# Query, key and value blocks in fp16 pairs by seven products, and the output projection in fp16

## The chip, the cores and the metric

The kernel runs on one core of a Trainium2 chip. The metric is the device time of one execution in microseconds. Of three runs of the kernel before, the median is 2335.99 us.

## What is computed

One layer of a decoder trunk for 512 tokens of 2048 features in f32: a token mixer (sparse attention with 16 heads in 4 groups), a squared-ReLU feed-forward part, a gated per-layer embedding add and a final norm. What matters here is the mixer:

```python
hn   = rms_norm(h, norm_mix)
proj = hn @ w_in          # q (16 x 128), kc, vc, ks, vs, kw, vw (4 x 128 each), 48 gates
k_cmp, v_cmp = compress(kc, ...), compress(vc, ...)      # silu(blk @ w1) @ w2
# for each head: three softmaxes over the same q: compressed, selected, window
out  = g0 * o_c + g1 * o_s + g2 * o_w
h    = h + out @ w_out
h    = h + (relu(rms_norm(h) @ ffn_w1) ** 2) @ ffn_w2    # 2048 -> 8192 -> 2048
h    = h + (p @ ple_w_proj) * sigmoid(rms_norm(h) @ ple_w_gate)
y    = rms_norm(h, norm_final)
```

With 512 tokens all eight selectable key blocks are selected, so the selected branch is causal attention over all tokens.

## The kernel before

Every product of f32 matrices is made from two halves of each factor, a high half (the value rounded to a shorter type) and a low half (what is left): `mm3` (L73) issues three matmuls, high by high, high by low and low by high, into one PSUM bank. Activations are kept transposed, features on partitions, so that a matmul has a 128x128 weight tile and up to 512 token columns. The type of the halves differs by stage:

- Attention stage, to about 850 us: halves in fp32r. `unit` (L105) loads a megabyte of weights (128 x 2048) and `halves` (L93) splits it; the high half is made on ScalarE (L79) and the low half on VectorE or, after the first projections, on GpSimd (L80, `lo_eng`).
- Feed-forward and embedding stages: halves in fp16, both scaled by a power of two that `scale_of` (L662) takes from a sum of squares (L676), made by `scaled_split` (L678). From the third group on, two blocks of `ffn_w1` are multiplied at once: a 2x2 partition of weights and inputs needs seven products of half-size blocks in place of eight (`PAIR`, `up_pair` L975), with 256 token columns in each matmul. `combos` (L942) makes the sums of input quarters, `prepare` (L716) those of the weights.

The attention stage runs so. The compression columns of keys (c = 0) and of values (c = 1) are projected first, 192 matmuls of 512 columns each, while the input is loaded, normed and split (`norm_split`, tiles ah and al, L160). Then follows one stream of jobs, made by `later_jobs` (L449): the compression itself (`cjob`, 130 columns), the gates, key and value blocks of each group and query blocks of each head (`block_job` L303, 48 matmuls into one bank, then `k_evac`, `v_evac` or `q_evac`), and output projections (`out_half` L290: 8 output tiles from two heads, each added to h at L299). `merge` (L472) interleaves that stream with the attention of the heads: `s_stage` (L333: scores, softmax, four row tiles; the first tile in the bank s1, the others in the bank pair s2) and `pv_stage` (L406: probabilities are transposed, split into th and tl, and multiplied with the values). A head's output oh, ol stands in fp32r.

In the later stages the weights are fed by a pump: `pump` (L753) is called after each used weight slot and decides on what is staged (loaded), squared, scaled and split next; RAWS = 6 raw buffers of 512 KB, SLOTS = 9 pairs of halves, `lags` the numbers of pumps between staging and squaring or scaling.

All this sets an order of priority. The order of each engine's instructions is then fixed when the program is built, by a planner that takes what is ready first (`TileContext(..., schedule_with_timeline_sim=True)`), so a later instruction can stand ahead of an earlier one that isn't ready. Engines run their instructions in that fixed order.

Of the kernel before, what the change touches and what calls it, by code (L numbers as in the profile page):

```python
# [31 lines left out]
SLOTS = 9  # L32
STD = 2
# [8 lines left out]
def trunk_kernel(ctx, tc, xT, pT, gains, w_kcvc, w_blk, w_gates, w_out, w1c, w2c, posT,  # L42
# [10 lines left out]
    wraw = a_sb.enter_context(tc.tile_pool(name="wraw", bufs=2))  # L53
    wsp = a_sb.enter_context(tc.tile_pool(name="wsp", bufs=3))
# [27 lines left out]
    lo_eng = [DVE]  # L82

# [9 lines left out]
    def halves(r, cols=2048, step=1024, pool=None, tags=("wh", "wl")):  # L93
        res = []
        for c in range(0, cols, 1024):
# [3 lines left out]
            for d in range(0, n, step):  # L99
                e = min(n, d + step)  # L100
                split(hi[:, d:e], lo[:, d:e], r[:, c + d:c + e], lo_eng[0])
# [11 lines left out]
    aconst = a_sb.enter_context(tc.tile_pool(name="aconst", bufs=1))  # L113
# [14 lines left out]
    wb = consts.tile([128, S], BF16, name="wb")  # L128
# [93 lines left out]
    def norm_scale(tag):  # L222
        rs = actp.tile([128, S], F32, name="rs", tag="rs")
        ACT.activation(rs, norm_bcast(tag), AF.Copy)
        return rs
# [20 lines left out]
    def gemm_k(o, hs, k, n=128):  # L246
        wh, wl = wslice(hs, k * n, n)
        mm3(o, wh, wl, ah[k], al[k], k == 0, k == NK - 1)

    warm = bank("pt")  # L250
    for i in range(WARM):
        mm(warm, wb[:, (i % 4) * 128:(i % 4 + 1) * 128], wb, True, True)
    kvp = a_sb.enter_context(tc.tile_pool(name="kv", bufs=1))
    A = {}

    def k_evac(o, rs, g, b, last):
        if b == 0:
            A["kx", g] = [kvp.tile([128, 1088], F32R, name=f"kx{e}", tag=f"kx{e}") for e in range(2)]
        kx = A["kx", g]
        t = tmp.tile([128, S], F32, name="kt", tag="t")  # L260
        DVE.tensor_mul(t, o, rs)
        for j in range(2):
            c0 = 32 + 544 * j
            d = [x[:, c0:c0 + 512].rearrange("p (j b n) -> p j b n", j=2, b=2)[:, :, b, :] for x in kx]
            split(d[0], d[1], t[:, j * 256:(j + 1) * 256].rearrange("p (j n) -> p j n", j=2))
# [5 lines left out]
    def v_evac(o, rs, g, b):  # L271
        t = tmp.tile([128, S], F32, name="vt", tag="t")
        DVE.tensor_mul(t, o, rs)
        vp = bank("pt")
        for i in range(4):
            nc.tensor.transpose(vp[:, i * 128:(i + 1) * 128], t[:, i * 128:(i + 1) * 128], ident)
        vh = kvp.tile([128, S], F32R, name="v_h", tag=f"vh{b}")
        vl = kvp.tile([128, S], F32R, name="v_l", tag=f"vl{b}")
        split(vh, vl, vp)
        A["vx", g, b] = (vh, vl)  # L280

    def q_evac(o, rs, hd):
        t = tmp.tile([128, S], F32, name="qt", tag="t")
        DVE.scalar_tensor_tensor(t, o, QSCALE, rs, op0=OP.mult, op1=OP.mult)
        qh = kvp.tile([128, S], F32R, name="q_h", tag="qh", bufs=2)
        ql = kvp.tile([128, S], F32R, name="q_l", tag="ql", bufs=2)
        split(qh, ql, t)
        A["q", hd] = (qh, ql)

    def out_half(pair, u, hs):  # L290
        os = [A["o", 2 * pair + e] for e in range(2)]
        for j in range(8):
            m = u * 8 + j
            o = bank("g")
            for e in range(2):
                wh, wl = wslice(hs, e * 1024 + j * 128)
                mm3(o, wh, wl, os[e][0], os[e][1], e == 0, e == 1)
                yield
            DVE.tensor_add(h[m], h[m], o)  # L299
            if pair == HEADS // 2 - 1:  # L300
                norm_sq(m, 12)

    def block_job(blk, evac, *a):  # L303
        def run(hs):
            o = bank("g")
            for k in range(NK):
                gemm_k(o, hs, k)
                if k == NK - 1:
                    evac(o, *a)
                yield  # L310
        return (lambda: unit(w_blk[blk]), run)

    def kjob(g, b):
# [935 lines left out]
```

## Time and profile before

| what | value |
|---|---|
| median of three runs | 2335.99 us (2334.61 to 2338.15) |
| the profiled execution, its own time | 2335.97 us |
| span of the profiled execution | 2334.0 us |
| TensorE busy | 2303.0 us |
| VectorE busy | 1562.6 us |
| ScalarE busy | 1285.7 us |
| GpSimd busy | 301.2 us |
| mean granted clock of TensorE | 0.995 |

PE is TensorE, PEld its weight load, DVE VectorE, ACT ScalarE, POOL GpSimd, SP the engine that issues the transfers. Times are from the start of the span. Busy times are unions of the records of one engine; the record of a matmul includes its way through the array, so that records of successive matmuls overlap, and the rate is read from the distance of their starts or from the length of a stretch. A name such as `wl<-raw,sc,wh` gives the tile written and those read; "idle before, releaser" says how long an engine stood idle before the group's instructions and who ended it.

### The profile page before, as it was taken

The page shows a single profiled execution, that of the slowest core. Times are in us where ns is not written, and L with a number is a line of the kernel's source. Part 1 is how long each engine was busy: PE and PEld are TensorE (multiplying, and loading weights), DVE is VectorE, ACT ScalarE, POOL GpSimd, SP SyncE. Part 2 cuts the span into 40 slices and gives each one's busy share as a digit, 9 for nine tenths or more (in the row PEclk, how much of TensorE's full clock was granted, in tenths as well). Part 3 has the DMA queues.
Part 4 walks back from the last instruction along what each step waited for, and adds up shares of the span by engine and source line. Part 5 has one row for each costly group of instructions (what it writes and reads, how often), then busy time and mean ns, then how long its engine had stood idle before and what let it go on. Part 6 is the DMA issues. An engine that isn't in the chain of part 4 may idle for free.

```text
span 2334.0 us, 35213 instructions
## 1 busy us (share of the span) xinstructions
PE 2303.0 (99%) x14042; PEld 1640.7 (70%) x14042; DVE 1562.6 (67%) x2752; ACT 1285.7 (55%) x2125; POOL 301.2 (13%) x161
## 2 busy tenths in 40 slices
PE   9999999999999989999999999999999999999997
PEld 7888888888888768577657766775677567644445
DVE  6447646646646958876777777677767776766733
ACT  5324434334333648576566656665666576565851
POOL 0243233232332120000000000000000000002012
PEclk9999999999999999999999999999999999999998
DMA  5232122222121413233233323333333233341411
GB/s 202 104 120 73 55 73 73 70 75 73 62 84 67 159 55 128 73 118 120 89 109 111 117 99 109 109 109 100 118 109 109 94 115 118 109 154 55 147 53 73
DMA packets 59061, 232.51 MB, mean 100 GB/s; under 512 B 6928, under 2 KB 7312, under 8 KB 51728
## 3 DMA queue, kind: packets, MB, share of 16 engines
q1 hardware_dynamic: 58896, 230.25, 29.4%
q8 instruction: 110, 1.80, 0.3%
q14 instruction: 55, 0.45, 0.1%
HBM read 223.94 MB, written 6.29 MB: 99 GB/s over the span
## 4 chain that ended last, share of the span: by engine, by line
PE 91%; DVE 4%; ACT 2%; DMA 2%; issue 1%; POOL 0%; SPq 0%; DVEq 0%; ACTq 0%; POOLq 0%
PE g_ps L71 50%; PE pt_ps L71 31%; PE s_ps L71 5%; PE o_ps L71 3%; PE pt_ps L427 1%; ACT s_ps L676 1%; DVE wl L683 1%; DVE xt L891 1%; DMA raw<-in_w_pg_dram 1%; ACT wh L682 1%; DMA raw<-in_ffn_dram 1%; DVE xgl L896 0%; PE pt_ps L419 0%; DVE p L384 0%; POOL fo L1178 0%
## 5 line engine op out<-in xcount | busy, mean ns | idle before, releaser
L71 PEld LDWEIGHTS <-wh 128*128 128x128 f16 x6336 | 609.0, 98 | 335.5 <-issue 8.8
L683 DVE SCALAR_TENSOR_TENSOR wl<-raw,sc,wh 128x1024 f16<-128x1024 f32 x266 | 341.6, 1288 | 188.3 <-ACT wh L682 184.5
L71 PEld LDWEIGHTS <-wl 128*128 128x128 f16 x3168 | 309.2, 98 | 174.4 <-issue 3.5
L676 ACT ACTIVATE s_ps<-raw 128x1024 f32<-128x1024 f32 x294 | 300.5, 1022 | 138.8 <-DMA raw<-in_ffn_dram 104.5
L682 ACT ACTIVATE wh<-raw,sc 128x1024 f16<-128x1024 f32 x266 | 298.5, 1139 | 90.0 <-PE g_ps L71 54.4
L80 POOL TENSOR_TENSOR wl<-raw,wh 128x1024 fp32r<-128x1024 f32 x100 | 240.6, 2411 | 506.0 <-ACT wh L79 496.0
L79 ACT ACTIVATE wh<-raw 128x1024 fp32r<-128x1024 f32 (+1 forms) x122 | 125.6, 1044 | 221.8 <-PE g_ps L71 160.1
L179 POOL TENSOR_TENSOR ssacc<-ssacc,sq 128x512 f32<-128x512 f32 x35 | 46.2, 1319 | 1428.8 <-issue 1289.8
L71 PE MATMUL g_ps<-ah,wh 128*128 128x512 f32 x544 | 215.4, 396 | 0.0
L71 PE MATMUL g_ps<-ah,wl 128*128 128x512 f32 x544 | 214.2, 394 | 0.0
L71 PE MATMUL g_ps<-al,wh 128*128 128x512 f32 x544 | 212.9, 391 | 0.0
L71 PE MATMUL pt_ps<-fh,wh 128*128 128x512 f16 (+1 forms) x544 | 203.1, 373 | 0.0
L71 PE MATMUL g_ps<-fh,wh 128*128 128x512 f16 (+1 forms) x544 | 203.0, 373 | 0.0
L71 PE MATMUL pt_ps<-fl,wh 128*128 128x512 f16 (+1 forms) x544 | 203.0, 373 | 0.0
L71 PE MATMUL g_ps<-fl,wh 128*128 128x512 f16 (+1 forms) x544 | 202.9, 373 | 0.0
L71 PE MATMUL g_ps<-fh,wl 128*128 128x512 f16 (+1 forms) x544 | 202.9, 373 | 0.0
L71 PE MATMUL pt_ps<-fh,wl 128*128 128x512 f16 (+1 forms) x544 | 202.8, 373 | 0.0
L683 DVE SCALAR_TENSOR_TENSOR wl<-S,sc,wh 128x1024 f16<-128x1024 f32 x112 | 143.6, 1282 | 76.1 <-ACT wh L682 73.4
L682 ACT ACTIVATE wh<-S,sc 128x1024 f16<-128x1024 f32 x112 | 127.5, 1139 | 72.2 <-PE pt_ps L71 39.6
L377 ACT ACTIVATE p<-s_ps,nm 128x128 f32<-128x128 f32 (+3 forms) x128 | 66.3, 523 | 116.2 <-DVE scm L373 57.3
L71 PE MATMUL pt_ps<-xcl,wh 128*128 128x256 f16 x448 | 122.2, 273 | 0.0
L71 PE MATMUL pt_ps<-xch,wh 128*128 128x256 f16 x448 | 122.1, 273 | 0.0
(286 smaller groups left out, 4880.7 us busy)
## 6 DMA issues: line engine op xcount, KB each, us to landing
raw<-in_ffn_dram SPq DMA_DIRECT2D x256, 512.0 KB, 3.8
raw<-in_w_blk_dram SPq DMA_DIRECT2D x32, 1024.0 KB, 4.8
raw<-in_w_out_dram SPq DMA_DIRECT2D x16, 1024.0 KB, 4.8
raw<-in_w_pg_dram SPq DMA_DIRECT2D x32, 512.0 KB, 3.8
h<-in_xT_dram SPq DMA_DIRECT2D x16, 256.0 KB, 6.6
raw<-in_w_kcvc_dram SPq DMA_DIRECT2D x4, 1024.0 KB, 4.8
raw<-in_w1c_dram SPq DMA_DIRECT2D x4, 1024.0 KB, 4.8
raw<-in_w_kcvc_dram SPq DMA_DIRECT2D x6, 512.0 KB, 6.3
```

Of the source, the lines that this page charges most:

```text
L71: nc.tensor.matmul(o, w, x, start=start, stop=stop, skip_group_check=True)
L79: ACT.activation(hi, src, AF.Copy)
L80: (eng or DVE).tensor_sub(lo, src, f32(hi))
L179: (DVE if e else eng or POOL).tensor_add(acc[e], acc[e], sq)
L377: ACT.activation(p, v[:, b], AF.Exp, bias=nm[:, b:b + 1], accum_out=r[:, b:b + 1])
L427: nc.tensor.transpose(pt[:, (i - kc) * 128:(i - kc + 1) * 128], A["P", hd, b, i, kc], ident)
L676: ACT.activation(junk, src, AF.Square, accum_out=sq)
L682: ACT.activation(hi[:, cs], src[:, cs], AF.Copy, scale=sc)
L683: DVE.scalar_tensor_tensor(lo[:, cs], src[:, cs], sc, hi[:, cs], op0=OP.mult, op1=OP.subtract)
L891: DVE.scalar_tensor_tensor(t, h[k], P["gx"][:, i, k:k + 1], rs, op0=OP.mult, op1=OP.mult)
```

## The change

- **Pairs.** The 32 key, value and query blocks are taken two at a time (`pair_job`): kk, vv and qq jobs, each by seven products of 256 token columns in fp16, as `up_pair` does. Products x and y go to the two g banks, v and u to the bank s1. The scale of the weights and of the norm's gain is taken out in the eviction.
- **Input quarters.** `pair_inputs` makes the fp16 halves of the input's quarters and of their combinations (7 pairs of tiles for each of 8 pairs of k-tiles) and writes them over ah and al, once the projection of c = 1 and the gates have read those. To free them in pairs, that projection runs over k in the order 0, 8, 1, 9, ... (`ORDER`), with the gates four k-tiles behind (`GLAG`).
- **Output projection.** `out_job` multiplies four heads at a time, in fp16: 4 jobs for each group, 4 output tiles in each, 4 x 3 matmuls into one bank, one scaled addition to h. oh and ol are written in fp16, with a scale from the values' squares (`o_scale`). The jobs of a group run beside the heads of the next; those of the last group come last.
- **Feed.** The pump becomes a class `Feed` with two instances: FF for the later stages as before, FA for attention (5 raw buffers, 4 slots, lags 1 and 3, sums of weights written in place). A pump of FA takes scales only where `scale` is true. `scale_of` takes one matmul and a VectorE sum in place of a matmul for each column.
- **Places.** All low halves are made on VectorE (`lo_eng` goes). The first score tile moves from bank s1 to s2. The first feed-forward weights are prepared beside the last group's output jobs.

```diff
+RAWS_A = 5
+SLOTS_A = 4
+LAGS_A = (1, 3)
+GLAG = 4
+ORDER = [k for p in range(8) for k in (p, p + 8)]
...
+    def scale_of(sq, n=1, pool=None):
...
+        mm(p[:, 0:c * n], wb, sq, True, True)
...
+        if c > 1:
+            src = pool.tile([128, 2], F32, name="se", tag="se")[:, 0:n]
+            DVE.tensor_reduce(src, p[:, 0:c * n].rearrange("p (c n) -> p n c", n=n), AX.X, OP.add)
...
+            for name in PAIR:
+                if self.inplace:
+                    if name == "S2":
+                        s1 = tile_s("S1")
+                        DVE.tensor_add(s1, a21, a22)
+                        DVE.tensor_add(a21, a21, a11)
+                        DVE.tensor_add(a11, a11, s1)
+                        S_.update({"S2": a11, "s3": a21})
+                    elif name == "S1":
+                        DVE.tensor_add(a12, a12, a11)
+                        S_["s4"] = a12
...
+                if scale and n < self.squared and self.pumps - items[n].at >= lags[1]:
+                    items[n].sc, items[n].inv = scale_of(items[n].sq, 1, self.p["sm"])
...
+    FA = Feed(PA, RAWS_A, SLOTS_A, True)
+    FA.lags = LAGS_A
...
+    def out_job(g, u):
+        it = FA.add(Item(w_out[g, u]))
...
+            for j in range(4):
+                m = 4 * u + j
+                o = bank("g")
+                for e in range(HPG):
...
+                    mm3(o, wh[:, ws], wl[:, ws], oh, ol, e == 0, e == HPG - 1)
...
+                DVE.scalar_tensor_tensor(h[m], o, iv, h[m], op0=OP.mult, op1=OP.add)
...
+    def pair_job(blk, evac, a0, a1, qs=1.0):
+        it = FA.add(Item(w_blk[blk], w_blk[blk + 1]))
...
+            def prod(b, w, x, first):
+                if first:
+                    o[b] = bank("g" if b in "xy" else "s1")
+                wh, wl = it.w[w]
+                for k in range(8):
...
+                    mm3(o[b][:, 0:H2], wh[:, ws], wl[:, ws], xh, xl, first and k == 0, k == 7)
...
+            yield from prod("x", "11", "11", True)
+            keep(1)
+            FA.used(False)
...
+            yield from prod("v", "12", "21", True)
+            total(0, 0, 1, "v")
+            FA.used(False)
...
+            yield from prod("x", "S2", "t2", False)
+            keep(2)
+            FA.used()
...
+            yield from prod("y", "S1", "t1", True)
+            FA.used()
...
+            yield from prod("x", "s3", "T3", False)
+            keep(3)
+            total(1, 1, 3, "y")
+            FA.used(False)
...
+            yield from prod("u", "22", "T4", True)
+            total(1, 0, 3, "u")
+            FA.used(False)
...
+            yield from prod("y", "s4", "22", False)
+            total(0, 1, 2, "y")
+            FA.used()
...
             if i == 0:
-                s = bank("s1")
+                s = sbank()
...
-        split(oh, ol, oc)
+        oh = opool.tile([128, S], F16, name="oh", tag=f"oh{hd % HPG}")
+        ol = opool.tile([128, S], F16, name="ol", tag=f"ol{hd % HPG}")
+        scaled_split(oh, ol, oc, A["osc", g][:, 0:1])
...
+    def pair_inputs(k):
+        ta, tb = xt(0, k, rs, tmp), xt(0, k + 8, rs, tmp)
...
+        xsplit(dh[:, 0], dl[:, 0], ta[:, 0:H2])
+        xsplit(dh[:, 1:3].rearrange("p a b -> p (a b)"), dl[:, 1:3].rearrange("p a b -> p (a b)"), tb)
+        cm = PA["S"].tile([128, 4, H2], F32, name="cm", tag="S")
+        combine(cm, ta, tb, ch, cl)
...
+    jobs = [kk_job(0), qq_job(0), vv_job(0)]
+    for g in range(GROUPS):
+        more = g + 1 < GROUPS
+        kinds = ["q2", 0, 1, "k", 2, "q4", "v", 3]
...
+    jobs += [out_job(GROUPS - 1, u) for u in range(4)]
...
+    merge([(s_stage(0, (pp, small)), 5)], 28, fill)
...
+        if r == HPG - 1 and more:
+            merge([(pvg, 10)], 28, fill)
+            flush()
+            merge([(s_stage(hd + 1, (pp, small)), 5)], 28 + no, fill)
+            flush()
         else:
...
+            gens = [(pvg, 10)] + ([(s_stage(hd + 1, (pp, small)), 5)] if hd + 1 < HEADS else [])
+            merge(gens, no + (28 if r == 0 else 14 if more else 0), fill)
...
+    merge([(early(12, 5), 12)], 64, fill)
```

## Rows read from the trace of the kernel before

**Rows 1.** Page, first section: busy us (share of span) and instructions.

```profile
PE 2303.0 (99%) x14042; PEld 1640.7 (70%) x14042; DVE 1562.6 (67%) x2752; ACT 1285.7 (55%) x2125; POOL 301.2 (13%) x161
```

**Rows 2.** Table by stage: length; busy PE, PEld, DVE, ACT, POOL; clock, DMA share, GB/s.

```profile
51.00:180.00 129.00, 129.00 (x682) 109.82 (x682) 57.16 (x83) 42.63 (x59) 48.93 (x21) 1.00 0.29 102
304.57:480.81 176.24, 176.23 (x882) 148.27 (x881) 108.34 (x218) 64.60 (x144) 57.77 (x25) 1.00 0.21 72
...
0.00:850.00 850.00, 838.93 (x4204) 699.64 (x4205) 523.57 (x1022) 345.05 (x700) 259.34 (x123) 1.00 0.26 90
```

**Rows 3.** Chain of waits in order of time: start, length, what.

```profile
108.06 5.31 PE s_ps L71 x48
...
362.28 12.05 PE g_ps L71 x53
...
938.37 0.03 PE s_ps L71 x2
938.39 10.50 PE g_ps L71 x96
...
2254.59 20.72 PE g_ps L71 x96
```

**Rows 4.** Groups of PE by line and shape: count, busy us, mean ns, idle before.

```profile
L71 PE MATMUL g_ps<-ah,wh 128*128 128x512 f32 x544 | 215.4, 396 | 0.0
...
L71 PE MATMUL g_ps<-ol,wh 128*128 128x512 f32 x256 | 100.4, 392 | 0.0
...
L71 PE MATMUL s_ps<-sq,wb 128*128 128x1 bf16 x310 | 36.4, 166 | 2.5 <-ACT s_ps L676 2.3
```

**Rows 5.** Timeline of 776 to 784 us: start, length, engine, line, operation.

```profile
776.98 4.78 POOL L80 TENSOR_TENSOR wl<-raw,wh 128x1024 fp32r<-128x1024 f32 x2 [15.61 <-ACT wh L79]
...
779.63 2.74 DVE L384 TENSOR_SCALAR p<-p,r,gate 128x384 f32<-128x384 f32 x2
...
783.08 1.27 DVE L299 TENSOR_TENSOR h<-h,g_ps 128x512 f32<-128x512 f32 x2
```

**Rows 6.** Groups of DVE by line and shape, from 845 us on.

```profile
L683 DVE SCALAR_TENSOR_TENSOR wl<-raw,sc,wh 128x1024 f16<-128x1024 f32 x257 | 330.4, 1288 | 188.1 <-ACT wh L682 184.3 <-PE g_ps L71 1.8
L1074 DVE SCALAR_TENSOR_TENSOR h<-g_ps,iv,h 128x512 f32<-128x512 f32 x128 | 95.4, 745 | 28.5 <-PE g_ps L71 28.5
...
L997 DVE TENSOR_TENSOR ft<-z,g_ps 128x256 f32<-128x256 f32 x84 | 32.4, 413 | 10.8 <-PE g_ps L71 9.2 <-PE s_ps L71 1.6
L669 DVE TENSOR_SCALAR e<-s_ps 128x1 int32<-128x1 int32 x131 | 19.7, 151 | 63.9 <-PE s_ps L71 63.9
```

**Rows 7.** Groups of DVE and POOL by line and shape, up to 845 us.

```profile
L299 DVE TENSOR_TENSOR h<-h,g_ps 128x512 f32<-128x512 f32 x126 | 84.9, 679 | 18.0 <-PE g_ps L71 17.8
L80 DVE TENSOR_TENSOR q_l<-qt,q_h 128x512 fp32r<-128x512 f32 x16 | 32.6, 2037 | 7.4 <-ACT q_h L79 7.4
...
L80 DVE TENSOR_TENSOR tl<-pt_ps,th 128x512 fp32r<-128x512 f32 x32 | 21.9, 685 | 9.7 <-ACT th L79 9.7
...
L80 POOL TENSOR_TENSOR wl<-raw,wh 128x1024 fp32r<-128x1024 f32 x100 | 240.6, 2411 | 506.0 <-ACT wh L79 496.0 <-PE g_ps L71 10.0
```

**Rows 8.** Groups of ACT by line and shape, up to 845 us.

```profile
L682 ACT ACTIVATE wh<-raw,sc 128x1024 f16<-128x1024 f32 x9 | 9.9, 1140 | 0.8 <-DVE sc L670 0.8
```

**Rows 9.** Page, DMA issues: count, KB each, median us from issue to landing.

```profile
raw<-in_ffn_dram SPq DMA_DIRECT2D x256, 512.0 KB, 3.8
```

**Rows 10.** Table by stage of four short stretches, columns as in the second group.

```profile
700.00:750.00 50.00, 50.00 (x261) 42.58 (x260) 39.06 (x89) 20.88 (x53) 13.50 (x6) 1.00 0.14 44
900.00:950.00 50.00, 49.61 (x454) 43.59 (x453) 45.99 (x96) 37.88 (x66) 0.00 (x0) 1.00 0.32 107
815.00:820.00 5.00, 2.31 (x11) 1.47 (x10) 5.00 (x6) 2.85 (x5) 0.00 (x0) 1.00 0.10 29
820.00:825.00 5.00, 5.00 (x20) 3.21 (x21) 0.07 (x2) 1.19 (x2) 0.00 (x0) 0.66 0.53 190
```

**Rows 11.** Waits of PE: line, who for, us in total, times, longest.

```profile
PE o_ps L71 <- DVE tl L80: 4.7, 3, 1.9
```

More of the change, by code (lines that the diff above doesn't have):

```diff
@@ L280, in v_evac @@
+        scaled_split(vh, vl, vp, sc)
         A["vx", g, b] = (vh, vl)
[L282 to L287, printed above, removed]
-        A["q", hd] = (qh, ql)
[L290 to L294, printed above, removed]
-            for e in range(2):
[L296 to L313, printed above, removed]
-        return block_job(g * 8 + b, k_evac, A["rs"], g, b, b)
-    def vjob(g, b):
-        return block_job(g * 8 + 2 + b, v_evac, A["rs"], g, b)
-    def qjob(hd):
-        return block_job((hd // HPG) * 8 + 4 + hd % HPG, q_evac, A["rs"], hd)
@@ L333, in s_stage, with kk_job, vv_job, qq_job @@
+    def kk_job(g):
+        return pair_job(g * 8, k_evac, (g, 0), (g, 1))
+    def vv_job(g):
+        return pair_job(g * 8 + 2, v_evac, (g, 0), (g, 1))
+    def qq_job(hd):
+        return pair_job((hd // HPG) * 8 + 4 + hd % HPG, q_evac, (hd,), (hd + 1,), QSCALE)
+    def stream(jobs):
+        for run in jobs:
+            yield from run()
     def s_stage(hd, pools):
@@ new lines, in trunk_kernel @@
+    hs = unit(w1c[1, 0])
+    for i in range(NK - GLAG, NK):
+        gate_step(i)
+    keep_kv(1, pss)
+    for i in range(NK - GLAG + 1, NK, 2):
+        pair_inputs(ORDER[i] - 8)
+    FA.pump()
+    compress(1, 0, hs)
+    hs = unit(w1c[1, 1])
+    compress_out(0)
+    gt = tmp.tile([128, S], F32, name="gt", tag="t")
+    DVE.tensor_mul(gt[0:96], gp[0:96, 0:S], rs[0:96])
+    FA.pump()
+    compress(1, 1, hs)
+    gates_out(gt)
+    compress_act(1)
+    for _ in range(12):
+        next(fill, None)
@@ L651, in trunk_kernel @@
+    compress_out(1)
+    c_sb.close()
+    P["kv"] = a_sb.enter_context(tc.tile_pool(name="kv", bufs=1))
+    for _ in range(16):
+        next(fill, None)
+    flush()
     pp = a_sb.enter_context(tc.tile_pool(name="pp", bufs=2))
@@ L674, in sum_sq @@
-    def sum_sq(junk, src, sq):
-        with nc.allow_low_precision(reason="a power of two is taken from it"):
-            ACT.activation(junk, src, AF.Square, accum_out=sq)
-    def scaled_split(hi, lo, src, sc, step=1024):
-        n = src.shape[-1]
-        for c in range(0, n, step):
-            cs = slice(c, min(n, c + step))
-            ACT.activation(hi[:, cs], src[:, cs], AF.Copy, scale=sc)
-            DVE.scalar_tensor_tensor(lo[:, cs], src[:, cs], sc, hi[:, cs], op0=OP.mult, op1=OP.subtract)
@@ L742, in trunk_kernel @@
             ms = [ffn1[G * FG + j] for j in range(FG)]
[L743 to L744 removed]
+            for it in [Item(a) for a in ms] if G < STD else [Item(*ms[0:2]), Item(*ms[2:4])]:
+                FF.add(it)
         if G > 0:
[L746 to L748 removed]
@@ L826, in trunk_kernel, with early @@
-    lo_eng[0] = POOL
-    merge([(s_stage(0, (pp, small)), 5)], counts[-1], fill)
+            for c in range(4):
+                FF.add(Item(ffn2[G - 1, c]))
+    for it in [Item(pT), Item(w_proj[1])] + [Item(w_pg[m]) for m in range(NK)]:
+        FF.add(it)
+    pump, used, take = FF.pump, FF.used, FF.take
+    def early(n0, n1):
+        FF.limit = n1
+        for n in range(n0):
+            FF.pump((1, 2))
+            yield
+    for _ in range(28):
+        next(fill, None)
+    flush()
@@ L925, in trunk_kernel @@
         for k in range(NK):
-            t = xt(0, k, rs)
+            t = xt(1, k, rs)
             if k < 8:
```

810 lines of the change are left out of this document (429 added, 381 removed).

## The prediction

> **What bounds the kernel now.** I read the page's first section, then the table by stage, then the chain of waits, then the groups of instructions on TensorE, VectorE and ScalarE. TensorE is busy 2303.0 of 2334.0 us [rows 1]. The part that the change rewrites is the attention stage, the first 850 us: TensorE works there for 838.9 us of 850, VectorE for 523.6 us, GpSimd for 259.3 us, and in a whole cycle of four heads (304.57 to 480.81) TensorE never waits while VectorE is busy 61% of the time [rows 2]. So time is saved by taking work from TensorE, as long as VectorE, which gets all that is added, keeps up. That is the whole question here: TensorE's saving is nearly certain, what is given back in waits isn't. The profiled execution took 2335.97 us, 2.0 more than its span, and the median is 2335.99; the sum below is a difference to either.
>
> **TensorE's work.** The rate is read from uninterrupted stretches of the chain, since the mean of a matmul's record includes its pipeline. 53 fp32r matmuls of 512 columns took 12.05 us, 0.2274 us each; 96 in fp16 of 512 columns 20.72 us, 0.2158 us each; 96 in fp16 of 256 columns 10.50 us, 0.1094 us each; 48 of 130 fp32r columns 5.31 us, 0.1106 us each [rows 3].
> - Query, key and value blocks: 32 blocks of 16 k-tiles by 3 matmuls are 1536 fp32r matmuls (three groups of 544, less the 32 of each that belong to the compression columns [rows 4]), 1536 x 0.2274 = 349.3 us. After: 16 pairs by 7 products by 8 k-tiles by 3 = 2688 matmuls of 256 columns, x 0.1094 = 294.1 us. Gain 55.2 us: 12.5% of it from seven products in place of eight, the rest from fp16.
> - Output projection: 768 matmuls (256 each of three groups [rows 4]) stay 768. 768 x (0.2274 - 0.2158) = 8.9 us.
> - Scales: 310 matmuls of one column [rows 4] become one for each scale, some 136 in the feed-forward stages and 39 new ones in attention. Two stretches of the chain are 0.03 us apart where two of them stand between [rows 3], so each costs between 0.015 and 0.1 us; at 0.025 the 135 fewer give 3.4 us (2 to 13).
> Attention itself, the compression and the gates have the same matmuls.
>
> The Trainium skill has a rule against halving the columns: TensorE: Matmul & The Clock Gate, section "Back-to-back issue gap", gives a sustained 131 ns for 512 columns and 81 ns for 128, hence, as an estimate on a line between, 98 ns for 256. By it the blocks would go from 201 to 263 us and the change would lose 62 us there. The trace disagrees: 0.2158 and 0.1094 us, a ratio of 0.51 [rows 3], so that of the rule only the mild form in the third rival is left.
>
> **VectorE's work in the attention stage.** Successive operations overlap by some 0.08 us (two of 0.68 us took 1.27 [rows 5]), so I take 0.08 off each mean [rows 6, 7].
> - A pair: 7 low halves of 1024 columns (1.288 - 0.08) and 4 sums of 1024, which I take as a little less (1.14), 4 totals of 256 (0.413 - 0.08), scale and factors about 0.45 (0.151 each less the overlap): 8.5 + 4.6 + 1.3 + 0.45 = 14.8 us, 16 times: 237 us [rows 6].
> - An output item: 2 low halves, 4 additions of 0.745, small ones: 5.5 us, 16 times: 88 us; 128 additions to h at 0.60 go: -77 us. The 32 scalings of evicted blocks go: -19 us [rows 6, 7].
> - Input quarters (pair_inputs), 8 times: two scaled copies of 512 (as the addition of 0.745), splits of 256, 512, 768 and 256 columns, four combinations of 256 (0.413): 1.3 + 2.2 + 1.3 = 4.8 us, together 39 us [rows 6].
> - Low halves of the compression weights move from GpSimd: 8 x 1.2 = 9 us.
> - GpSimd's 100 subtractions of 2411 ns go from this stage, and with them a collision: q_l, with both inputs in SBUF, took 2037 ns, tl of the same size but with one input in PSUM 685 [rows 7]; while GpSimd worked from 776.98 on, p took 2.74 us for two [rows 5]. For q_l alone this is 16 x 1.35 = 22 us; over all groups of such operations some 80 us, an estimate (22 to 90).
> The sum: 523.6 + 237 + 88 - 77 - 19 + 39 + 9 - 80 and some small ones = about 715 us, while TensorE's becomes 838.9 - 55.2 - 8.9 + 1 = 776 us. VectorE goes from 62 to 92% of TensorE's time. ScalarE's added work (1.140 us for each high half, about as much for each square [rows 8]) makes it some 75% busy and isn't the bound.
>
> On the collision the Trainium skill, GPSIMD Engine Reference, section "Key points", says that GpSimd shares its SBUF interfaces with VectorE and collides with instructions of two SBUF inputs or a two-port mode. By that rule the 80 is right rather than the 22, as p and the small vectors would be freed too.
>
> **Where TensorE will wait.**
> 1. *The start.* From 51 us on, TensorE has 192 x 0.2274 + 32 x 0.2274 (gates) + 192 x 0.1106 (compression) = 72 us until the first pair. In that time VectorE must make the quarters (39), 16 low halves (19), the two evictions of compression inputs (10), activations, gates and the first two weight slots (about 9): 77 us at least. The last eviction, two of the eight pair_inputs and the last compression weights all come after the last projection matmul, when TensorE has only about 12 us left to cover 17 to 20. Before, nothing waited here (129.00 of 129.00 [rows 2]). I take 13 us, bounds 4 and 20.
> 2. *The end of each pair.* The scale of the next item may only be taken in pumps with `scale` true and three pumps after it was staged; it is staged after the second product (before that the five raw buffers are full), so the first such pump is the one after the seventh product. All weights of the pair are used by then. Then the chain stands bare: scale matmul 0.2, four small VectorE operations 0.6 (0.151 each), the high half 1.14, the low half 1.29: 3.2 us [rows 4, 6, 8]. Sixteen pairs: 51 us if nothing covers it, 0 if attention's matmuls, which are merged into the same stream, always do. The trace of before has no such place, as its weights lie up to nine slots ahead. Five ends have little attention queued (the first two pairs, and the last query pair before each value pair, where the scores wait for that query's own eviction): 5 x 3.2 = 16 us. At the other eleven about 1.9 us of ready attention work stands in the queue: 11 x 1.3 = 14 us. I take 30, the middle of the bounds for the reason given. The load isn't on this chain: 5 products are 13 us, and four transfers of 512 KB, 3.8 us from issue to landing [rows 9], overlap.
> 3. *The clock.* In 815 to 820 TensorE worked 2.31 of 5 us, and in the next 5 us its granted clock was 0.66 [rows 10], a mean of the levels 2.4 and 1.2 GHz, so 1.7 us were lost. Waits of 3 us should do this at some of the sixteen places: I take 5 us (0 to 27).
> 4. *Thin heads.* Heads 13 to 15 get one output item each (48 x 0.2158 = 10.4 us) beside them, and all four score tiles now share one bank pair: 3 us (0 to 8).
> 5. *Waits that go.* The waits for tl, 4.7 us in three, the longest 1.9 [rows 11], come from VectorE late by the collision (p's 2.74 us stands right before that one [rows 5]): -5 us (-6 to 0). The feed-forward stages and the end keep their order; hence nothing.
>
> Sum: -55.2 - 8.9 - 3.4 + 13 + 30 + 5 + 3 - 5 = -21.5 us, 2314.5 us.
>
> **Rivals.**
> *The waits are covered.* The order of instructions is made by readiness, so later attention work can fill the 3.2 us gaps; VectorE's idle time in a cycle of four heads is 176.24 - 108.34 = 68 us now [rows 2], which speaks for it. Then only 5 us of the start and 2 of the thin heads stay: -67.5 - 5 + 7, 2270 us. Against it: the first two pairs have no attention beside them at all. Chance 0.22.
> *VectorE becomes the bound: slower.* It must do 715 us in order while TensorE's waits depend on it. The point of decision is the share at which it can be kept busy: at 715/850 = 0.84 the stage is as long as before. The best 50 us of before are 45.99, or 0.92, in the feed-forward stage, which speaks against; the best within attention are 39.06, or 0.78 [rows 10], though VectorE waited for TensorE there. At 0.82 the stage takes 872 us: +22, less 3.4, about 2354 us. Chance 0.18.
> *The fp16 products don't run at their rate between fp32r matmuls.* If each costs half an fp32r matmul, 0.1137 us [rows 3], the blocks gain 43.7 and the output little: the sum is some -1, 2335 us. The mixed stretches of attention, where 512-column fp32r matmuls keep to 0.23 us, speak against. Chance 0.07.
>
> **How the numbers follow.** The forecast, 2314, has 0.53, with 2297 to 2333 as its own range. The range of all: the covered case lies at 2270, with half of its chance above 2275, and a mild case of the VectorE bound ends at 2348: 2275 to 2348. A measurement tells 0.2% (4.7 us) from no change, so "same" is 2331.3 to 2340.7. Faster: 0.47 of the forecast, the 0.22, 0.02 of the VectorE case, 0.02 of the third: 0.73. Slower: 0.01 of the forecast, 0.14 of the VectorE case, 0.02 of the third: 0.17. Same: the rest, 0.10.
>
> **What would show it.** Right: 2688 matmuls of 256 columns 0.109 us apart; VectorE 700 to 730 us busy in the attention stage; TensorE idle 2 to 4 us before the first product of pairs, on VectorE's wl or ScalarE's wh, and some 10 us before the first pair; q_l back at about 0.7 us; cycles of four heads of 160 to 170 us in place of 176.2. Wrong: TensorE's idle time within 10 us of before (the gaps were covered), or waits for tl and the score tiles spread over all heads (VectorE's queue is the bound), or a feed-forward cycle that differs from 78.5 us by more than 1 us.

## Result and the profile after

| | before | after |
|---|---|---|
| median, us (four runs each) | 2335.84 | 2353.39 (2351.41 to 2354.33) |
| ratio to before, 95% interval | | 1.0071 (1.0058 to 1.0084) |
| span of the profiled execution, us | 2334.0 | 2351.0 |
| mean granted clock | 0.995 | 0.981 |

The change makes the kernel 0.7% slower; forecast were 2314 us and a range that ended at 2348. The page's first section after, to be read against [rows 1]:

```profile
PE 2270.4 (97%) x15094; PEld 1558.6 (66%) x15094; DVE 1756.5 (75%) x3345; ACT 1487.2 (63%) x2474; POOL 60.1 (3%) x61
```

TensorE is busy 32.6 us less, and yet the end comes 17 us later. To see how much of its busy time is work, I took the distance from each matmul's start to the next one's in both traces, and its median for each form at the full clock. Median times count is the time that the work needs; the rest of the distances is idle time, what is lost while the granted clock is at 1.2 GHz, and small delays of matmuls that overlap their neighbours' records:

| us, whole trace | before | after | difference |
|---|---|---|---|
| work at the full clock | 2286.3 | 2219.4 | -66.9 |
| TensorE idle | 21.5 | 71.3 | +49.8 |
| lost at the low clock | 6.2 | 33.3 | +27.1 |
| small delays | 9.8 | 17.1 | +7.3 |

So the matmuls save what was forecast (-67.5), and 84 us come back as waits and clock, where 46 were forecast. The table by stage after shows where (columns as in [rows 2]):

```profile
100.00:121.00 21.00, 14.38 (x65) 11.11 (x63) 19.58 (x42) 10.98 (x18) 0.00 (x0) 0.88 0.15 50
121.00:172.00 51.00, 40.07 (x278) 32.52 (x278) 38.74 (x76) 22.16 (x38) 0.00 (x0) 0.81 0.14 42
172.00:205.00 33.00, 25.06 (x192) 20.01 (x193) 20.94 (x35) 17.24 (x27) 0.00 (x0) 0.90 0.21 64
205.00:480.00 275.00, 262.40 (x1964) 211.85 (x1962) 245.38 (x542) 185.24 (x385) 0.00 (x0) 0.97 0.22 68
480.00:700.00 220.00, 213.36 (x1539) 162.93 (x1537) 185.48 (x399) 144.17 (x287) 0.00 (x0) 0.97 0.25 79
700.00:800.00 100.00, 99.95 (x624) 67.65 (x623) 83.85 (x205) 63.98 (x132) 0.00 (x0) 1.00 0.33 111
800.00:900.00 100.00, 87.79 (x491) 53.23 (x491) 62.57 (x129) 63.08 (x112) 15.64 (x12) 0.93 0.20 69
...
0.00:850.00 850.00, 795.37 (x5347) 612.05 (x5348) 702.22 (x1492) 542.84 (x1042) 14.35 (x20) 0.96 0.28 91
```

Of the 84 us, 39 arise between 100 and 205 us, where before nothing waited: idle 25.5, clock 11.3, small delays 2.8. Another 32 arise from 205 to 800 us, 6.5 from 800 to 900, and some 6 in the feed-forward and embedding stages, of which the forecast said nothing. VectorE is busy 702.2 of the first 850 us, 523.57 before [rows 2].

What TensorE waits for, first from 100 to 205 us, then ("...") from 205 to 700 us (who for: us in total, times, longest):

```profile
PE g_ps L80 <- ACT wh L285: 6.7, 3, 4.3
PE g_ps L80 <- DVE c L551: 4.8, 2, 2.9
PE s_ps L80 <- DVE vst L829: 3.7, 1, 3.7
PE s_ps L80 <- DVE kcmp L89: 2.6, 1, 2.6
...
PE s_ps L80 <- ACT p L642: 6.4, 6, 3.9
PE pt_ps L692 <- DVE v_l L286: 2.6, 2, 1.5
PE o_ps L80 <- ACT th L88: 1.9, 3, 1.0
PE g_ps L80 <- ACT wh L285: 1.6, 2, 0.8
...
PE s_ps L80 <- ACT wh L285: 1.2, 3, 0.4
```

There is no one waiter: the pair's weights (wh), the pair's totals (c), the compression's last copies (vst, kcmp) and attention's own steps (p, th, v_l) are all late at times. The compression's small steps stand one behind the other across three engines: from 150 to 172 us TensorE waits 6.9 us while VectorE itself is busy less than half of the time:

```profile
150.00:172.00 22.00, 15.07 (x98) 11.17 (x95) 10.38 (x26) 8.42 (x19) 0.00 (x0) 0.84 0.21 71
```

The end of the first pair (its product u comes last there), from the timeline (start, length, engine, line, operation, idle before and its releaser), is the bare chain that was forecast:

```profile
170.70 0.31 PE L80 MATMUL s_ps<-xch,wl 128*128 128x256 f16 x1
171.04 0.42 DVE L551 TENSOR_TENSOR c<-zs,s_ps 128x256 f32<-128x256 f32 x1 [4.55 <-PE s_ps L80]
...
171.52 0.16 PE L80 MATMUL s_ps<-sq,wb 128*128 128x4 bf16 x1 [0.51 <-DVE c L551]
171.72 0.16 DVE L265 TENSOR_REDUCE se<-s_ps 128x1 f32<-128x4 f32 x1 [0.25 <-PE s_ps L80]
...
172.51 0.14 DVE L268 TENSOR_SCALAR sc<-e 128x1 int32<-128x1 int32 x1
172.63 2.19 ACT L285 ACTIVATE wh<-raw,sc 128x1024 f16<-128x1024 f32 x2 [0.62 <-DVE sc L267]
...
173.83 0.28 PE L80 MATMUL g_ps<-xdh,wh 128*128 128x256 f16 x1 [2.15 <-ACT wh L285]
```

From 171.01, the end of the pair's last matmul, to 173.83 TensorE does one scale matmul and waits 2.7 us. The scale matmul itself waits for the total c, since both use the bank s1.

The clock, in five short stretches (columns as above):

```profile
117.00:122.00 5.00, 0.62 (x3) 0.13 (x2) 5.00 (x13) 3.99 (x4) 0.00 (x0) 0.50 0.00 0
293.00:297.00 4.00, 2.30 (x14) 1.57 (x13) 3.44 (x14) 2.69 (x11) 0.00 (x0) 1.00 0.00 0
297.00:300.00 3.00, 3.00 (x13) 2.76 (x13) 2.47 (x8) 2.21 (x3) 0.00 (x0) 0.51 0.02 5
498.00:502.00 4.00, 2.68 (x13) 1.64 (x13) 4.00 (x9) 2.85 (x7) 0.00 (x0) 0.55 0.02 4
502.00:506.00 4.00, 4.00 (x23) 2.99 (x23) 4.00 (x8) 2.19 (x2) 0.00 (x0) 0.59 0.00 0
```

From 293 to 297 us TensorE waited 0.71, 0.58 and 0.41 us, no wait of a whole microsecond; the clock fell to 1.2 GHz at 297.1 and stayed there for 3.4 us, in which TensorE worked without a pause. At 498.4 us it fell after waits of 0.16, 0.61 and 0.26 us in the 2.8 us before, and stayed low for 6.8 us; the waits of 0.80 and 0.43 us in the row from 498 us came with and after the fall. In the first 900 us there are 16 such stretches, 75 us together; before there were two.

### The profile page after: what moved, and what is told of

Same layout as the page of the kernel before. It is cut to its first block, busy times and chain, and to the rows that moved or that the text cites. A ratio compares the mean times of both kernels' runs of the same rounds, so it can differ in the third digit from the quotient of the medians.

```text
span 2351.0 us, 38233 instructions
## 1 busy us (share of the span) xinstructions
PE 2270.4 (97%) x15094; PEld 1558.6 (66%) x15094; DVE 1756.5 (75%) x3345; ACT 1487.2 (63%) x2474; POOL 60.1 (3%) x61
## 4 chain that ended last, share of the span: by engine, by line
PE 75%; DVE 12%; DMA 6%; ACT 4%; issue 3%; POOL 0%; ACTq 0%; DVEq 0%; POOLq 0%
PE g_ps L80 36%; PE pt_ps L80 30%; PE s_ps L80 5%; DVE wl L286 3%; DMA raw<-in_w_blk_dram 3%; PE o_ps L80 2%; ACT wh L285 1%; DMA raw<-in_ffn_dram 1%; DMA raw<-in_w_pg_dram 1%; ACT s_ps L273 1%; DMA raw<-in_w_out_dram 1%; DVE xt L740 1%; DVE nm L636 1%; PE pt_ps L692 1%; DVE p L649 1%
## 5 line engine op out<-in xcount | busy, mean ns | idle before, releaser
L80 PEld LDWEIGHTS <-wh 128*128 128x128 f16 x8640 | 839.2, 99 | 464.4 <-issue 29.0
L286 DVE SCALAR_TENSOR_TENSOR wl<-raw,sc,wh 128x1024 f16<-128x1024 f32 x394 | 505.0, 1285 | 192.6 <-ACT wh L285 186.7
L80 PEld LDWEIGHTS <-wl 128*128 128x128 f16 x4320 | 425.6, 99 | 225.6 <-issue 8.1
L285 ACT ACTIVATE wh<-raw,sc 128x1024 f16<-128x1024 f32 x394 | 442.1, 1140 | 132.1 <-PE g_ps L80 69.0
L80 PE MATMUL g_ps<-xch,wh 128*128 128x256 f16 x832 | 226.8, 273 | 0.0
L80 PE MATMUL g_ps<-xcl,wh 128*128 128x256 f16 x832 | 226.6, 273 | 0.0
L80 PE MATMUL g_ps<-xch,wl 128*128 128x256 f16 x832 | 225.2, 273 | 0.0
L273 ACT ACTIVATE junkA<-raw 128x1024 bf16<-128x1024 f32 x96 | 101.4, 1057 | 76.0 <-DMA raw<-in_w_blk_dram 49.2
L80 PE MATMUL pt_ps<-xch,wl 128*128 128x256 f16 x448 | 122.1, 272 | 0.0
L1219 DVE SCALAR_TENSOR_TENSOR h<-g_ps,iv,h 128x512 f32<-128x512 f32 x128 | 95.4, 745 | 25.0 <-PE g_ps L80 25.0
```

Of the source, the lines that this page charges most:

```text
L80: nc.tensor.matmul(o, w, x, start=start, stop=stop, skip_group_check=True)
L273: ACT.activation(junk, src, AF.Square, scale=sc, accum_out=sq)
L285: ACT.activation(hi[:, cs], src[:, cs], AF.Copy, scale=sc)
L286: DVE.scalar_tensor_tensor(lo[:, cs], src[:, cs], sc, hf, op0=OP.mult, op1=OP.subtract)
L1219: DVE.scalar_tensor_tensor(h[m], o, iv, h[m], op0=OP.mult, op1=OP.add)
```

## Experiments

Differences in this table are to the kernel after, from the ratios: (ratio - 1.0071) x 2336 us. The interval of a single ratio is 0.0010 to 0.0022 to either side, 2.3 to 5 us; with the kernel after's own interval a difference is uncertain by 4 to 6 us.

| run | ratio to before | us against after |
|---|---|---|
| e1_const: fixed weight scale | 0.9979 (0.9970 to 0.9989) | -21.5 |
| e2_flag6: scale one product earlier | 1.0103 (1.0087 to 1.0120) | +7.5 |
| e3_quarters: seven of eight pair_inputs left out | 1.0045 (1.0030 to 1.0060) | -6.1 |
| e4_nolow: no low halves of the weights | 0.9957 (0.9943 to 0.9972) | -26.6 |
| e5_start: other bank, two buffers | 1.0064 (1.0049 to 1.0079) | -1.6 |
| e6_junk: squares to SBUF | 1.0157 (1.0142 to 1.0172) | +20.1 |
| e8_fill: 224 idle matmuls added | 1.0092 (1.0075 to 1.0109) | +4.9 |
| e9_nosq: e1 without squares | 0.9944 (0.9924 to 0.9963) | -29.7 |
| e10_all: e9 and e4 | 0.9810 (0.9793 to 0.9826) | -61.0 |
| e11_all_q: e10 and e3 | 0.9763 (0.9749 to 0.9778) | -71.9 |
| e12_pact: e9, softmax scaling on ScalarE | 0.9932 (0.9911 to 0.9954) | -32.5 |
| e14_nop: no softmax scaling | 1.0035 (1.0024 to 1.0047) | -8.4 |

### The scale chain

```diff
+                if hasattr(self, "fixed") and n < self.staged:
+                    items[n].sc, items[n].inv = self.fixed[:, 0:1], self.fixed[:, 1:2]
+                    self.scaled += 1
+                    continue
```

> The kernel after, but the attention stage's weights (pairs and output items) take a fixed scale of 64 in place of the one from their squares; the squares are still made, only the scale matmul and its four VectorE operations of each item are left out, so a weight slot can be split as soon as its load has landed. Theory 1 (the chain scale, high half, low half stands bare at the end of each pair and at the start): the waits of 0.6 to 4 us before the first products of a pair go, and with them most of the 75 us at the low clock: 30 to 45 us less, 2308 to 2323 us. Theory 2 (the start is bound by VectorE, the pair ends cost little): -3 to -12 us, 2341 to 2350. Theory 3 (VectorE's queue as a whole is the bound): only 32 times 0.6 us of VectorE's work go, most of it hidden: -5 to -15 us, 2338 to 2348.

Measured: 2330.61 us, 21.5 us less. The chain costs time, half to three quarters of the 30 to 45 us that the theory of bare chains expected. Its profiled execution took 2337.70 us, 7 more than its median, so its trace isn't read for shares. It does show that the waits of the start changed their names here too: from 100 to 205 us none for wh is left, and the longest two are for the compression's copies:

```profile
PE g_ps L80 <- DVE kct L787: 8.7, 1, 8.7
PE s_ps L80 <- DVE vst L836: 4.8, 1, 4.8
```

```diff
             total(1, 0, 3, "u")
-            FA.used(False)
+            FA.used()
```

> The kernel after, with one flag changed: a scale may also be taken in the pump after a pair's sixth product, so that the chain of the next pair starts one product (24 matmuls, 2.6 us) earlier; the same work. Theory 1: the bare chain of 3.2 us at a pair's end gets 2.6 us of cover; at 16 ends -10 to -30 us with the clock that comes back, 2323 to 2343 us. Theory 2: only the ends in the start matter, -2 to -5 us, about 2350. Theory 3: within 4 us of the kernel after, since VectorE's work is the same.

Measured: 2360.90 us, slower, which no theory expected. From 200 to 900 us TensorE now waits for zs, ScalarE's copy of product x out of its bank, 6.2 us (the kernel after: 0.7 us):

```profile
PE g_ps L80 <- ACT zs L548: 6.2, 6, 2.0
```

Ahead of each of the six, ScalarE runs a high half of later weights (wh) or a square (junkA) and goes on to zs without a pause; here at one of the two longest:

```profile
521.42 2.18 ACT L285 ACTIVATE wh<-raw,sc 128x1024 f16<-128x1024 f32 x2
523.50 1.05 ACT L273 ACTIVATE junkA<-raw 128x1024 bf16<-128x1024 f32 x1
...
524.53 0.37 ACT L548 ACTIVATE zs<-g_ps 128x256 f32<-128x256 f32 x1
```

So work for later weights stands ahead of zs in ScalarE's fixed order; this is some 5 of the 9.4 us that TensorE idles more from 205 to 700 us (PE 466.33 us busy for 475.75). That the earlier scale put it there fits, but no run tests it. Starting the chain earlier doesn't help by itself.

### Work taken from VectorE and ScalarE

```diff
+            if self.inplace:
+                ACT.activation(hi, src, AF.Copy, scale=it.sc)
+                it.w[name] = (hi, hi)
+                return
```

> The kernel after, without the low halves of the attention stage's weights (pairs and output items): the products take the high half in both places, as many matmuls as before; 144 VectorE operations of 1.25 us are left out, 180 us. Theory 3 (VectorE's queue as a whole bounds the stage): nearly all of the waits go, 55 to 75 us less, 2278 to 2298 us. Theory 1: the chain at a pair's end loses only its last link, 1.3 of 3.2 us, at 16 ends: 15 to 25 us less with some clock, 2328 to 2338. Theory 2: in the start 14 low halves fewer, 10 to 18 us less, 2335 to 2343.

Measured: 2325.62 us, 26.6 us less: within its interval no more than the 15 to 25 us of a shorter chain, and less than half of what a hard bound would give. Some 11 of the 26.6 us stand in the start, where TensorE begins 636 matmuls from 100 to 205 us in place of 535. This run alone doesn't tell the first theory from a softer form of the third; the next one is meant to.

```diff
-                DVE.tensor_scalar(p, p, r[:, b:b + 1], gate[:, i, 3 * hd + 1 + b:3 * hd + 2 + b],
-                                  op0=OP.mult, op1=OP.mult)
```

> The kernel after without the scaling of the softmax rows (128 VectorE operations of 0.44 us, 56 us, spread over the heads; the probabilities stay unscaled); the weights' scales, squares and low halves are as in the kernel after. Theory A (leaving out the low halves helped because VectorE's queue as a whole is shorter): the same gain for each microsecond, 28 us for 180, so some 9 us less, 2340 to 2347 us. Theory B (it helped because the low half is the last link of the chain ahead of a pair's first product): 0 to 3 us less, 2350 to 2354 us.

Measured: 2345.16 us, 8.4 less. This work stands in no pair's chain, yet each microsecond of it is worth about as much as one of the low halves: 8.4/56 = 0.15 (0.08 to 0.22 by the intervals), 26.6/180 = 0.15 (0.12 to 0.17). So VectorE's queue counts beyond the pairs' chain. It does stand in attention's chain from scores to transposes; that this chain got shorter is a rival that no run excludes, though no wait of TensorE for this scaling is among those of the kernel after from 205 to 700 us. The table by stage from 205 to 700 us, of the kernel after, e14_nop, e4_nolow and e10_all in this order:

```profile
205.00:700.00 495.00, 475.75 (x3500) 374.79 (x3498) 430.86 (x940) 329.41 (x672) 0.00 (x0) 0.97 0.23 73
...
205.00:700.00 495.00, 476.94 (x3539) 374.23 (x3538) 402.62 (x845) 332.82 (x681) 0.00 (x0) 0.98 0.23 73
...
205.00:700.00 495.00, 479.89 (x3628) 380.61 (x3626) 322.14 (x861) 336.49 (x697) 0.00 (x0) 1.00 0.24 76
...
205.00:700.00 495.00, 491.56 (x3677) 389.54 (x3676) 328.75 (x804) 279.19 (x573) 0.00 (x0) 0.99 0.25 85
```

VectorE is busy 430.86 of 495 us in the kernel after, 0.87, while TensorE works 0.96 of the time. With 322 us (e4) the clock is back at 1.00, but TensorE still waits 15 us; only when the scale chain and the squares are gone as well (e10) do the waits fall to 3.4 us.

```diff
+                    if not hasattr(self, "fixed"):
                         self.square(items[n])
```

> The run with fixed weight scales (e1_const) without the squares as well: 96 ScalarE operations of 1.06 us and as many reads of their sums (0.19 us) are left out, 120 us of ScalarE's 540 in the attention stage. Theory A (ScalarE's order is a bound of its own: TensorE's longest waits in the run with fixed scales are on ScalarE's zs, p and th): 12 to 30 us less than that run, 2300 to 2318 us. Theory B (VectorE's queue is the bound, and ScalarE waits for it too): within 5 us of that run, 2325 to 2336 us.

Measured: 2323.20 us, 8.2 less than e1_const for 120 us of ScalarE's work, 0.07 each (0.03 to 0.11); between the two theories.

```diff
-                DVE.tensor_scalar(p, p, r[:, b:b + 1], gate[:, i, 3 * hd + 1 + b:3 * hd + 2 + b],
-                                  op0=OP.mult, op1=OP.mult)
+                ACT.activation(p, p, AF.Copy, scale=r[:, b:b + 1])
```

> The run with fixed scales and no squares (e9_nosq) with the scaling of the softmax rows (128 operations of 0.44 us, 56 us) moved from VectorE to ScalarE, one scale for each row made by a small VectorE operation. Theory A (VectorE's queue is what TensorE still waits for between 205 and 900 us, ScalarE has room since the squares went): 5 to 15 us below that run, 2308 to 2318 us. Theory B (the order of work on ScalarE is as tight: its p, zs and th end the longest waits there): 0 to 10 us above it, 2323 to 2333 us.

Measured: 2320.30 us, 2.8 less than e9_nosq, within the intervals of both. The theories aren't told apart; whether the work costs as much on ScalarE as on VectorE stays open. With e9_nosq's edit it beats both kernels, if a fixed scale of 64 may be relied on for the weights.

> Three reliefs at once: fixed weight scales, no squares of the attention stage's weights, and no low halves of them (the products take the high half in both places); as many matmuls as in the kernel after, less 32 scale matmuls. Theory A (the bare chains and the busy queues of VectorE and ScalarE are separate causes): the gains seen alone, some 30 us and 28 us, add up: 2290 to 2300 us. Theory B (they shorten the same chain, high half then low half ahead of the next product, and shadow each other): 2306 to 2320 us. In both the start, 100 to 205 us, keeps more than 20 of its 39 us of idle time and low clock.

Measured: 2292.52 us, 61.0 less; the two gains alone sum to 56. They add up, as theory A has it: neither relief hides the other. That the start keeps 20 us of its 39 was wrong: by the sums of starts it kept 17.8.

### The start

```diff
+        if k:
+            for n in ("t1", "T4", "T3", "t2", "11", "21", "22"):
+                XA[n, k] = XA[n, 0]
+            return
```

> The kernel after, with the input quarters and their combinations made for the first pair of k-tiles only and used for all eight (seven of eight pair_inputs are left out, 38 us of VectorE's work between 85 and 130 us, nothing else). Theory 2 (the start, 100 to 200 us, is bound by VectorE's work on the quarters): the idle time of 24 us and the low clock there shrink by more than half, 18 to 35 us less, 2318 to 2335 us. Theory 1: the first pairs still end on bare chains and only the wait before the first pair shrinks: 4 to 10 us less, 2343 to 2349. Theory 3: 38 us of some 700 us of VectorE's work go, all of them gained if VectorE bounds the stage throughout: about 2315, and the waits after 200 us stay as they are.

Measured: 2347.23 us, 6.1 less. The trace doesn't show this gain in the start: by 205 us TensorE has begun 1053 matmuls where the kernel after has begun 1047, and by 900 us 5663 for 5656. It shows it between 2100 and 2300 us, where there is no edit; first the kernel after, then e3_quarters:

```profile
2100.00:2300.00 200.00, 193.40 (x916) 88.38 (x915) 109.30 (x208) 122.15 (x181) 29.61 (x23) 1.00 0.26 83
...
2100.00:2300.00 200.00, 197.57 (x937) 90.57 (x936) 110.57 (x210) 122.46 (x182) 30.33 (x23) 1.00 0.26 83
```

The kernel after waits there 4.0 us for squares of weights, in three waits that e3 and e5 don't have. So VectorE's quarters alone don't bound the start, and the 6.1 us are no price of VectorE's work; what removes those three waits wasn't tried.

```diff
-        op = bank("s1")
+        op = bank("pt")
...
-        gq = bank("s1")
+        gq = bank("pt")
...
-                hr = st_pool.tile([128, 4, NB], F32, name="hr", tag="hr")
+                hr = tmp.tile([128, 4, NB], F32, name="hr", tag="t")
```

(vhi and e likewise.)

> The kernel after, same work, with the small products of the compression and the gates (compress_out, gates_out) in a pt bank in place of s1, and the serial copies behind them (tag hr) in two buffers in place of one. Theory A (the start waits for the bank s1: the pair's product u waits 3.7 us until the four copies vst <- vhi are through, and the first scale matmul 2.6 us for kcmp): both waits go and the clock recovers with them: 6 to 14 us less, 2339 to 2347 us. Theory B (the start is bound by VectorE's queue and by late loads, the bank is only where the wait shows): within 3 us of the kernel after, 2350 to 2356, and the same idle time turns up at the next product.

Measured: 2351.69 us, the same as the kernel after within its interval; in its trace the first 900 us are some 5 us longer (5609 matmuls begun for 5656), and the stretch from 2100 to 2300 us is shorter, as in e3. The waits for vst and kcmp are gone from the list of 100 to 205 us, and these stand at its head:

```profile
PE g_ps L80 <- DVE c L551: 8.0, 2, 4.5
PE g_ps L80 <- ACT wh L285: 7.0, 4, 4.2
PE pt_ps L80 <- DVE kct L780: 5.4, 1, 5.4
```

The compression's copies stand ahead of the pair's total c in VectorE's order, so the wait moved from one to the other: the bank was only where it showed. No run puts c ahead of the copies.

> The run e10_all with the input quarters made for the first pair of k-tiles only as well (seven of eight pair_inputs left out). Theory A (the start is several chains of like length beside each other: VectorE's quarters, the compression's small copies, the splits of the first weights; taking one alone gave 6 us): together they give 15 to 30 us below e10_all. Theory B (the start hangs on one chain that none of these touches, the small copies of the compression in order on VectorE): 3 to 8 us below e10_all, as it was alone.

Measured: 2280.51 us, 10.9 less than e10_all (5 to either side), between the two theories. Here the gain does stand in the start (810 matmuls from 100 to 205 us for 725): the quarters are worth some 0.29 us for each of their microseconds when the other chains are short, and nothing that the trace shows when not. The table from 100 to 205 us, of the kernel after, e3_quarters, e10_all and e11_all_q:

```profile
100.00:205.00 105.00, 79.51 (x535) 63.64 (x534) 79.26 (x151) 50.38 (x81) 0.00 (x0) 0.85 0.16 51
...
100.00:205.00 105.00, 88.20 (x540) 73.53 (x539) 61.67 (x111) 43.18 (x67) 0.00 (x0) 0.79 0.16 50
...
100.00:205.00 105.00, 93.67 (x725) 80.08 (x725) 74.49 (x150) 53.56 (x87) 0.00 (x0) 0.95 0.23 75
...
100.00:205.00 105.00, 98.63 (x810) 86.79 (x809) 58.70 (x122) 50.40 (x85) 0.00 (x0) 1.00 0.24 78
```

Without the quarters alone TensorE waits 8.7 us less here and has begun only 5 matmuls more, since its clock is lower (0.85 to 0.79, against 105.00 us at 1.00 before). So waits and low clock can stand in each other's place where something else sets the time, and the clock's share of the start's loss need not be a loss of its own. Only all four reliefs together bring the clock to 1.00 and the idle time to 6.4 us.

### The clock

```diff
+            def prod(*a):
+                yield from prod0(*a)
+                for _ in range(16 if pad is not None else 0):
+                    mm(pad[:, 0:128], wb, wb, True, True)
```

> The kernel after with added work of no use: 16 matmuls of 128 bf16 columns (0.053 us each at the full clock, half of what they take in the first 6 us) behind each of the seven products of the first two pairs, 12 us of TensorE time between 121 and 200 us. Theory A (the low clock of these stretches follows from TensorE's own waits, so filling them brings it back): the 30.7 us at the low clock between 100 and 205 fall below 20, the padding lies in waits to the larger part, and the time is within 6 us of the kernel after, 2347 to 2359 us. Theory B (the clock falls for another reason): the low stretches stay and the padding is paid in full, 2362 to 2367 us.

Measured: 2358.11 us, 4.9 more for 12 us of added matmuls. The stretches at 1.2 GHz between 100 and 205 us fell from 30.7 to 17.1 us, the mean clock there rose to 0.92 from 0.85:

```profile
100.00:205.00 105.00, 85.82 (x742) 73.57 (x740) 76.64 (x148) 48.81 (x76) 0.00 (x0) 0.92 0.15 51
```

So the low clock follows from TensorE's own waits. Filling them gave back some 7 of the 12 us that it cost, at the edge of the interval.

### The thin heads

```diff
+        if hd == HEADS - HPG:
+            P["junk"] = PA["junk"]
```

> The kernel after, same work, but the squares of the feed-forward stage's weights write their unused result to an SBUF tile in place of the score bank pair s2. Theory A (thin heads: at 800 to 820 us four score tiles, and these squares, share one bank pair, and TensorE waits for it): the waits there (1.6, 2.3 and 2.5 us, with 13.7 us at the low clock) go, 5 to 10 us less, 2343 to 2348 us. Theory B (there ScalarE itself is late, 63 of 100 us busy, or the loads are): within 3 us of the kernel after.

Measured: 2372.57 us, 20.1 more. From 800 to 820 us TensorE's waits fell by only 1.7 us (7.6 to 5.9) and changed their names. The loss is in the feed-forward stage, about a microsecond in each of its cycles:

```profile
PE pt_ps L80 <- ACT z L1141: 14.0, 14, 1.4
```

ScalarE now idles 160.4 us for loads from 1100 to 1900 us, where it was 71.0 in the kernel after. This fits squares that stand earlier in ScalarE's order, ahead of their loads, with z, which TensorE needs, behind them; that the score bank had held them back is read from these waits, and no run tests it.

## Why the prediction was wrong, step by step

- **TensorE's work.** Right: -66.9 for -67.5. The medians of the distances are 0.227, 0.216 and 0.109 us, as in [rows 3], so the third rival (fp16 not at its rate) falls. (Of the 55.2 us forecast for the blocks, seven products in place of eight give 43.7, 12.5% of 349.3 and not of the gain, as the prediction has it.) The trace speaks against the sustained figures of the Trainium skill (TensorE: Matmul & The Clock Gate, "Back-to-back issue gap") here too.
- **VectorE's work.** Right in sum: 702.2 us busy for 700 to 730 (the terms as written add up to 720.6, not 715). Of the 80 us taken off for GpSimd, q_l shows 21 and the scaling of softmax rows 18 (69.4 to 51.1); the rest isn't shown. q_l, 2037 ns before [rows 7], takes as long as an operation that GpSimd doesn't disturb, which agrees with the Trainium skill's rule on the shared interfaces (GPSIMD Engine Reference, "Key points"); no run here put GpSimd back:

```profile
L286 DVE SCALAR_TENSOR_TENSOR q_l<-c,ivp,q_h 128x512 fp32r<-128x512 f32 x16 | 11.6, 744 | 0.0
```

- **The start.** Too small. 13 us, and two bare pair ends of 3.2, were forecast; measured are 28.3 us of idle time and small delays, and 11.3 of clock. The step that failed is the overlap: the sum held VectorE's work against TensorE's as totals. In the trace the quarters, the splits, the compression's copies and the pair's totals stand in one order on VectorE, and TensorE waits now for one, now for another (e5, e11), even where VectorE isn't full (150 to 172 us). The loads, which the prediction put off a pair's chain, are late too from 100 to 205 us, and no run brings them earlier:

```profile
ACT junkA L273 <- DMA raw<-in_w_blk_dram: 7.7, 7, 2.9
```

- **The ends of pairs.** The mechanism is there once, at the end of the first pair (2.7 us bare at 171 us). From 205 to 800 us idle time and small delays rose by 18.7 us, where the other pair ends, less the tl waits, were to give 18.6: the number agrees by luck. Of the 19.3 us of idle time there only some 3 end with the pair's weights, none of these waits is longer than 0.8 us, and the sign of 2 to 4 us before the first product of a pair is missing; most ends with attention's own steps (p, v_l, th, q_h). The scale chain does cost time, 21.5 us by e1, but as one of several things in one order and not as a bare wait at each pair's end.
- **The clock.** The term that was short by most: 5 us forecast, 27.1 measured, 22 of the 38 us that the sum was short. I let some of sixteen waits of 3 us pull it down, from one example [rows 10]; in fact waits of 0.41 to 0.71 us close together were followed by the low clock too (297 us). It was the upper end of my own bounds (0 to 27), yet the range took the bounds of the terms as if they were independent of each other, while new waits and low clock came together. As e3 shows, low clock can take the place of waiting in the start, so the 27 us are a part of the account and not a cause apart from the waits.
- **Thin heads.** Idle time from 800 to 900 us rose by 3.7 us, forecast 3. e6 took the squares out of the shared bank pair without a gain; that the four score tiles share it wasn't tested, so the cause is open.
- **"The feed-forward stages keep their order; hence nothing."** Wrong by some 6 us: the cycle is 78.3 us against 78.5, as forecast, but scale matmuls wait longer for squares whose loads come late:

```profile
PE s_ps L80 <- ACT s_ps L273: 7.3, 6, 1.8
```

  This is from 900 to 2300 us; it was 1.6 us there in the kernel before. Of the 7.3 us 4.0 stand from 2100 to 2300 us, and they come and go with edits elsewhere (e3, e5). Why the loads come later wasn't tried.
- **Four-head cycles.** 167.3 us (498.40 to 665.70), in the range of 160 to 170:

```profile
498.40:665.70 167.30, 164.06 (x1177) 124.08 (x1177) 144.47 (x313) 110.11 (x221) 0.00 (x0) 0.98 0.24 76
```

  So the steady part gains 9 us a cycle, and the loss lies in the start, in the first cycle and in the clock.
- **The rival "VectorE becomes the bound" gave 2354 us, and 2353.4 came.** Its time was met by luck, and its mechanism is half right. It said that VectorE can't be kept busier than 0.82; it was busy 0.87 of 495 us. A bound in its sense would return a microsecond for each that is taken away; some 0.15 came back (e4, e14). What fits is softer: each added microsecond on VectorE makes some result later, and a part of these delays reaches TensorE. As a rough estimate, with these prices taken for the whole stretch, the added 179 us on VectorE at 0.15, 198 us on ScalarE at 0.07 ([rows 2] and the same stretch of the kernel after; 345.05 us before) and 21.5 us for the chain give 62 us, of 78 that the first 900 us lost.

## What to carry to other kernels

The engine that sets the time lost 66.9 us of work, as forecast; the work that this put on other engines was not free below their limits. Here, as estimates, VectorE at 0.87 cost some 0.15 us for each microsecond (e4, e14) and ScalarE at 0.67 about half of that (e9), but the quarters alone cost nothing that e3's trace shows in the attention stage: count a price for added work, not only a limit, and expect it to differ from place to place. Where matmuls ran without a pause, add something for the clock to every new wait: here 50 us of new waits came with 27 us of low clock. In e1 and e5 the waits that one change removed were replaced by others behind work of the same engines, so ask whose order a wait stands in, and don't go by the name in the list of waits.

## What was not expected of the hardware

- Three waits of 0.41 to 0.71 us within four microseconds, in which TensorE worked 2.30 us, were followed by 3.4 us at 1.2 GHz (297.1 us); waits of 0.16, 0.61 and 0.26 us by 6.8 us (498.4 us, and much the same at 665.7).
- Of two runs of which one waits 8.7 us less in the start, the one with less waiting had the lower mean clock there (0.79 against 0.85): the sum of the waits alone doesn't tell the clock.
- The squares cost about the same with their result in SBUF as in PSUM, 1057 and 1023 ns for 1024 columns (1100 to 1900 us), so their length doesn't explain the 20 us of e6.
